# One GpSimd instruction for each token's second scatter factor

## The chip, the cores and the metric

The kernel runs on one core of a Trainium2 chip. The metric is the device time of one execution in microseconds (us). A core has five engines that run side by side, each through its own list of instructions in a fixed order: TensorE (PE, with its weight loads as PEld), VectorE (DVE), ScalarE (ACT), GpSimd (POOL) and SyncE (SP). SP, ACT and POOL also issue DMA transfers, and such an issue has its place in the engine's list.

## The reference, cut to what matters

The program is one decoder layer on 1,024 tokens of 1,024 features. A first half (projections, gating, a state space model, an output projection) ends in a residual `x`. The second half retrieves experts. Each token has 8 heads. For each head the token is scored against two lists of 128 keys, the best 16 of both lists give 16 experts out of 128 x 128, and a softmax gives their gates:

```
top_s, top_i = lax.top_k(s, PEER_TOPK)
cand_i = top_i[:, :, 0, :, None] * PEER_NKEYS + top_i[:, :, 1, None, :]
best_s, pos = lax.top_k(cand_s, PEER_TOPK)
idx = jnp.take_along_axis(cand_i, pos, axis=-1)
g = jax.nn.softmax(best_s, axis=-1)
act = jax.nn.gelu(jnp.einsum('thkd,td->thk', u_tab[idx], t))
return jnp.einsum('thk,thkd->td', g * act, v_tab[idx])
```

So each token has 128 slots (8 heads x 16), each with a row index i, a column index j (expert 128*i + j) and a gate g.

## The kernel before, in words

The tokens form eight blocks of 128. Blocks 5 to 7 take the sparse way: their experts' rows are gathered from memory by POOL's indirect DMAs (L871, L882), which run all through the last part of the program. Blocks 0 to 4 take the dense way: all 16,384 experts are computed for them by matmuls (`stage1`, tiles `pa`, and `stage2`, tiles `res` and `pd`), and each token's gates must first stand in a dense table `G_d` of 128 x 128 numbers for each token.

That table is made by `scatter`, the function that the change touches. For each token two factors are built, with the token's 128 slots on the partitions. `a1` has a one at column i of each slot (L679, one DVE instruction for four tokens). `b1` has the gate g at column j of each slot. One matmul of the two (L689, tile `pgs`, one for each token, two records in the trace) sums over the slots and gives the token's 128 x 128 table. ACT copies eight tokens' tables from PSUM to `GS` (L692), and SP writes `GS` to `G_d`. In 640 tokens (five blocks) this makes 160 `a1`, 640 `pgs` matmuls and 160 copies.

Before the change `b1` takes two steps. For eight tokens DVE makes a one-hot `hot` in 16-bit floats (L674). Then, for most pairs of tokens, ACT multiplies the one-hot by the gate, one instruction for each token (L687); for every 6th, 9th or 2nd pair, as the list `dv` in `CFG` says for the block, DVE does it for the pair (L683). There are six `b1` tiles of two tokens each, and two `a1` tiles of four.

Around the scatter runs `route`, DVE's search for the best keys of one block (`topk`: MAX8, FIND_INDEX8 and MATCH_REPLACE8 on tiles `m`, `ixs`, `scr`, `bs`, `po`, `ca`, then lookups on `mk`). Blocks 0 to 4 need their route before their scatter, blocks 5 to 7 need it for their gathers. When the last `GS` lies in `G_d`, the tables `Gt` are loaded, `weigh` multiplies them into the activations `w`, and `stage2` begins.

The order on each engine comes in two steps. The list `plan` in `CFG` gives each part of the work (r5 for route of block 5, s3 for scatter of block 3) a start and a length, which set the order in which the parts are written. Then a scheduler of the framework, which reckons with its own durations of the instructions, may move instructions within each engine's list. On the chip each engine keeps its list.

Of the kernel before, what the change touches and what calls it, by code (L numbers as in the profile page):

```python
# [15 lines left out]
AF = mybir.ActivationFunctionType  # L16
ALU = mybir.AluOpType
# [4 lines left out]
P = 128  # L22
# [15 lines left out]
NE = 128  # L38
QG = 4
FMAX = 3.0e38  # L40
CFG = dict(xo=[2, 3, 4, 0, 1], gt=3, ss=7, hs=2, b1=6, nw=11, raw=1, ngb=3, rows=6, lead=5, per=6, dv=[6, 9, 9, 2, 99], early=2,
           hp=600, eo=(2, 4), em={2: 'pppxx', 4: 'Xpp'}, seg=4, plan=dict(
    op0=(-238.2, 44.5), sb0=(-21, 248.8), m5=(-490.1, 3.4), r0=(234.1, 82.1), op1=(132.1, 27.3), op2=(292.7, 7.7),
    sb1=(310, 10.8), op3=(364.9, 36.8), r1=(301.9, 79), s0=(261.5, 137.5), sb2=(303.2, 61.7), zv=(372.6, 16.7),
# [3 lines left out]
    gt=(858.2, 122), rel=(739, 334), s4=(981.8, 131.5), r5=(916.4, 58.6), r6=(989.9, 124.6), ld=(776, 675.7),  # L48
# [47 lines left out]
@with_exitstack  # L96
def tile_hybrid_layer(ctx: ExitStack, tc: tile.TileContext, a, out, cfg=CFG):
    nc = tc.nc
    V, A, G, T = nc.vector, nc.scalar, nc.gpsimd, nc.tensor
# [70 lines left out]
    def slotS(shape, name, dt=F32):  # L170
        return sS.tile(shape, dt, tag="k8", name=name)
# [36 lines left out]
    early = {}  # L208
# [341 lines left out]
    ss = []  # L550
# [93 lines left out]
        bc2 = sm.tile([P, D], F32, tag="x", name="bc2", bufs=3)  # L644
        nc.scalar.dma_start(gt2_d, row_bcast(bc2, mod[5], "gt2"))

    gx = kp = sC = tk = iot = iot8 = None

    def slotC(shape, name, dt=F32):
        return sC.tile(shape, dt, tag="k8", name=name)  # L650

    def mid():
        nonlocal gx, kp, sC, tk, iot, iot8
        sB.release()
        gx = ctx.enter_context(tc.tile_pool(name="gx", bufs=1, side="left"))
        kp = tc.alloc_tile_pool(name="tk", bufs=1, side="left")
        sC = tc.alloc_tile_pool(name="sC", bufs=4, side="right")
        tk = topk_consts(tc, kp)
        iot = kp.tile([P, P], F32, name="iot")
        G.iota(iot, pattern=[[1, P]], base=0, channel_multiplier=0, allow_small_or_imprecise_dtypes=True)  # L660
        iot8 = kp.tile([P, P, 8], F16, name="iot8")
        G.iota(iot8, pattern=[[1, P], [0, 8]], base=0, channel_multiplier=0, allow_small_or_imprecise_dtypes=True)
        yield

    tops = {}

    def scatter(b, I32t, J16, gT):
        t0 = b * P
        for q in range(4):
            GS = [slotS([P, NE // 2, 32], f"GS{b}_{q}_{i}") for i in range(2)]  # L670
            for t8 in range(4):
                s1 = q * 32 + t8 * 8
                hot = kp.tile([P, P, 8], F16, tag="hs", name=f"hot{b}_{s1}", bufs=cfg["hs"])
                V.tensor_tensor(hot, iot8, bcast(J16[:, s1:s1 + 8], 1, P), op=ALU.is_equal)  # L674
                pg = bankB(f"pgs{b}_{s1}")
                for o in range(8):
                    if o % 4 == 0:
                        a1 = kp.tile([P, 4, P], F32, tag="a1", name=f"a1_{b}_{s1 + o}", bufs=2)
                        V.tensor_tensor(a1, bcast(iot, 1, 4), bcast(I32t[:, s1 + o:s1 + o + 4], 2, P), op=ALU.is_equal)  # L679
                    if o % 2 == 0:  # L680
                        b1 = kp.tile([P, 2, P], F32, tag="b1", name=f"b1_{b}_{s1 + o}", bufs=cfg["b1"])
                        if (s1 + o) // 2 % cfg["dv"][b] == 0:
                            V.tensor_tensor(b1, hot[:, :, o:o + 2].rearrange("p j t -> p t j"),  # L683
                                            bcast(gT[:, s1 + o:s1 + o + 2], 2, P), op=ALU.mult)
                        else:
                            for n in range(2):
                                A.activation(b1[:, n], hot[:, :, o + n], AF.Copy,  # L687
                                             scale=gT[:, s1 + o + n:s1 + o + n + 1])
                    T.matmul(pg[:, o // 4, (o % 4) * P:(o % 4 + 1) * P], b1[:, o % 2], a1[:, o % 4], start=True, stop=True)  # L689
                pgv = pg.rearrange("p a (t i) -> p i (a t)", t=4)  # L690
                for i in range(2):
# [58 lines left out]
    def route(b):  # L750
        if b < NDB:
            sc = scs.pop(b)
            get = lambda h: sc[:, h]
        else:
            part = {}

            def get(h):
                if h % 2 == 0:
                    part[0] = kp.tile([P, 2, 2, P], F32, tag="hs", name=f"scr{b}_{h}", bufs=cfg["hs"])
                    nc.sync.dma_start(part[0], sc_d[b - NDB, :, h:h + 2])  # L760
                return part[0][:, h % 2]

        i32, j16, g = yield from topk(tc, kp, tk, get, b)
        if b >= NDB:
            gi = gx.tile([P, NS], F32, name=f"gw{b}")
            ix = gx.tile([P, NS], I32, name=f"ix{b}")
            V.tensor_copy(gi, g)
            fi = kp.tile([P, NS], F32, tag="fi", name=f"fi{b}")
            V.scalar_tensor_tensor(fi, i32, 128.0, j16, op0=ALU.mult, op1=ALU.add)
            V.tensor_copy(ix, fi)  # L770
            tops[b] = ix, gi
        else:
            ij = kp.tile([P, 2, NS], F32, tag="ij", name=f"ij{b}")
# [262 lines left out]
    def prep_steps(n):  # L1036
# [17 lines left out]
        gt=(gt2_row, 1, "m5"), rel=(release, NDB, "gt op7 sb7"), ld=(lambda: lead(0, L), 2 * L, "rel"))  # L1054
# [13 lines left out]
    while left:  # L1068
# [3 lines left out]
        _, n, need = items[item]  # L1072
# [383 lines left out]
```

## Time and profile before

| what | value |
|---|---|
| median of 3 runs | 2688.28 us (2676.6 to 2693.47) |
| profiled execution, first to last instruction (span) | 2681.3 us |
| profiled execution's own time beside the span | none is given; the median run is 7.0 us above the span |
| PE busy | 2549.5 us, 95% |
| DVE busy | 2302.3 us, 86% |
| ACT busy | 903.2 us, 34% |
| POOL busy | 1038.4 us, 39% |

The busy shares are means over very different stretches. The scatter runs from 357 us (first `hot`) to 857.7 us (last copy to `GS`); after it comes the long loop over the experts, up to the end. POOL does nothing at all between 340 and 860 us, and its busy time is almost all in the loop's gathers. "Releaser" in a row is what ended an engine's idle time.

### The profile page before, as it was taken

What the parts mean: (1) busy time and instruction counts of PE and PEld (TensorE: products, weight loads), DVE (VectorE), ACT (ScalarE), POOL (GpSimd) and SP (SyncE); (2) the same over time, 40 slices, a digit from 0 to 9 for tenths busy, and PEclk for the clock granted to TensorE, in tenths of its full rate; (3) what the DMA queues carried; (4) which work ended last, traced back from release to release, by engine and by line L of the source; (5) the groups of instructions that cost most, each with busy time, mean ns of one, the idle gap of its engine ahead of it and who ended that gap; (6) DMA issues with size and microseconds to landing.
All of it is one profiled execution on the core that took longest, in us unless ns stands there. A gap on an engine that the chain in (4) does not pass through costs nothing.

```text
span 2681.3 us, 39165 instructions
## 1 busy us (share of the span) xinstructions
PE 2549.5 (95%) x14119; PEld 2171.5 (81%) x14119; DVE 2302.3 (86%) x5013; ACT 903.2 (34%) x1612; POOL 1038.4 (39%) x842
## 2 busy tenths in 40 slices
PE   6999999999878999999999999999999999999995
PEld 2557676588667898999889999888998899998894
DVE  7984699869899888888898988789897889888998
ACT  2311246578877422222222222222222222222222
POOL 0001000000000255566665665556565456555662
PEclk9996999999997999999999999999999999999998
DMA  9646232342545699999999999989999899998995
GB/s 351 114 151 181 101 134 103 111 157 111 200 139 198 236 348 316 324 330 330 330 359 342 344 332 324 331 312 345 335 341 333 301 330 368 336 332 305 353 322 201
DMA packets 298115, 724.76 MB, mean 270 GB/s; under 512 B 42384, under 2 KB 133008, under 8 KB 292384
## 3 DMA queue, kind: packets, MB, share of 16 engines
q0 software_dynamic: 112832, 411.09, 41.9%
q1 hardware_dynamic: 88800, 254.48, 26.6%
q10 hardware_dynamic: 96288, 56.69, 7.5%
q8 instruction: 111, 1.82, 0.3%
q14 instruction: 84, 0.69, 0.1%
HBM read 658.60 MB, written 62.39 MB: 269 GB/s over the span
## 4 chain that ended last, share of the span: by engine, by line
PE 24%; issue 23%; DVE 21%; POOL 15%; DMA 10%; ACT 5%; POOLq 0%; ACTq 0%; DVEq 0%
POOL rv L882 12%; PE pa L927 6%; DVE jk L874 4%; DMA Gt<-G_d 4%; PE pd L973 4%; POOL ru L871 3%; ACT b L687 3%; PE res L964 3%; PE pq L724 2%; PE po L626 2%; PE pgs L689 2%; DMA ru<-in_peer_u_dram,ix 1%; ACT GS L692 1%; PE pzs L360 1%; DMA vr<-in_peer_v_dram 1%
## 5 line engine op out<-in xcount | busy, mean ns | idle before, releaser
L927 PE MATMUL pa<-Th,u 128*128 128x320 f32 x4096 | 912.4, 310 | 8.7 <-DVE acc L981 5.3
L871 POOL DMA_INDIRECT ru<-in_peer_u_dram,ix x384 | 503.2, 1310 | 1016.4 <-issue 702.0
L927 PEld LDWEIGHTS pa<-Th,u 128*128 128x128 f32 x4096 | 688.3, 188 | 13.5 <-issue 3.3
L882 POOL DMA_INDIRECT rv<-in_peer_v_dram,ix x384 | 515.0, 1341 | 341.7 <-DVE gacc L887 271.1
L927 PE MATMUL pa<-Tl,u 128*128 128x320 f32 x2048 | 634.3, 310 | 0.0
L973 PE MATMUL pd<-v,wh 128*128 128x512 f32 x1536 | 482.4, 392 | 17.0 <-ACT v L913 6.9
L887 DVE SCALAR_TENSOR_TENSOR gacc<-rv,act,gacc 128x1024 f32<-128x1024 f32 x381 | 487.7, 1280 | 8.0 <-DMA rv<-in_peer_v_dram,ix 5.1
L874 DVE CUSTOM_DVE_ANT_0 jk<-ru,hn 128x1024 bf16<-128x1024 f32 x384 | 468.0, 1219 | 14.0 <-DMA ru<-in_peer_u_dram,ix 10.8
L927 PEld LDWEIGHTS pa<-Tl,u 128*128 128x128 f32 x2048 | 385.8, 188 | 1.2
L973 PEld LDWEIGHTS pd<-v,wh 128*128 128x128 f32 x1536 | 288.3, 189 | 81.8 <-ACT v L913 10.7
L964 PE MATMUL res<-v,wh 128*128 128x512 f32 x1024 | 319.4, 390 | 0.8 <-ACT wh L949 0.8
L973 PE MATMUL pd<-v,wl 128*128 128x512 f32 x768 | 299.9, 391 | 0.2 <-DVE wl L950 0.2
L946 DVE TENSOR_TENSOR w<-w,Gt 128x320 f32<-128x320 f32 x256 | 123.6, 483 | 184.7 <-DMA Gt<-G_d 181.4
L905 ACT CAST u<-ur 128x1024 fp32r<-128x1024 f32 x128 | 134.4, 1050 | 429.2 <-PE pd L973 231.1
L949 ACT CAST wh<-w 128x640 fp32r<-128x640 f32 x128 | 93.1, 728 | 492.7 <-DVE w L946 492.4
L687 ACT ACTIVATE b<-hot,gT 128x128 f32<-128x128 f16 x520 | 233.0, 536 | 59.5 <-PE pgs L689 40.2
L689 PE MATMUL pgs<-a,b 128*128 128x128 f32 x1280 | 191.0, 302 | 43.3 <-DVE a L679 21.0
L689 PEld LDWEIGHTS pgs<-a,b 128*128 128x128 f32 x1280 | 172.5, 210 | 65.2 <-ACT b L687 32.7
L964 PEld LDWEIGHTS res<-v,wh 128*128 128x128 f32 x1024 | 192.1, 188 | 40.7 <-ACT wh L949 1.2
L929 ACT ACTIVATE w<-pa 128x320 f32<-128x320 f32 x256 | 109.5, 434 | 281.5 <-PE pa L927 228.3
L964 PE MATMUL res<-v,wl 128*128 128x512 f32 x512 | 199.2, 390 | 1.4 <-DVE wl L950 1.4
L973 PEld LDWEIGHTS pd<-v,wl 128*128 128x128 f32 x768 | 144.8, 188 | 31.0 <-DVE wl L950 0.6
(348 smaller groups left out, 2994.5 us busy)
## 6 DMA issues: line engine op xcount, KB each, us to landing
vr<-in_peer_v_dram SPq DMA_DIRECT2D x128, 512.0 KB, 7.1
ur<-in_peer_ut_dram SPq DMA_DIRECT2D x128, 512.0 KB, 7.1
G_d<-GS SPq DMA_DIRECT2D x40, 1024.0 KB, 5.9
Gt<-G_d ACTq DMA_DIRECT2D x64, 640.0 KB, 16.4
wada<-in_w_ada_dram SPq DMA_DIRECT2D x17, 1024.0 KB, 13.3
wo<-in_w_out_dram SPq DMA_DIRECT2D x8, 1024.0 KB, 4.9
ru<-in_peer_u_dram,ix POOLq DMA_INDIRECT x384, 7.2
rv<-in_peer_v_dram,ix POOLq DMA_INDIRECT x384, 7.3
```

The costliest lines, as they stand in the source:

```text
L687: A.activation(b1[:, n], hot[:, :, o + n], AF.Copy, scale=gT[:, s1 + o + n:s1 + o + n + 1])
L689: T.matmul(pg[:, o // 4, (o % 4) * P:(o % 4 + 1) * P], b1[:, o % 2], a1[:, o % 4], start=True, stop=True)
L871: G.indirect_dma_start(out=row, out_offset=None, in_=a["peer_u"], in_offset=bass.IndirectOffsetOnAxis(ap=ix[:, s:s + 1], axis=0))
L874: V.tensor_tensor_reduce(out=junk, in0=row, in1=hn, scale=1.0, scalar=0.0, op0=ALU.mult, op1=ALU.add, accum_out=act[:, s:s + 1])
L882: G.indirect_dma_start(out=row, out_offset=None, in_=a["peer_v"], in_offset=bass.IndirectOffsetOnAxis(ap=ix[:, s:s + 1], axis=0))
L887: V.scalar_tensor_tensor(ac, row, act[:, s:s + 1], ac, op0=ALU.mult, op1=ALU.add)
L905: A.copy(u[:, 0], ur)
L927: T.matmul(pa[:, :NN], l[:, k, :], r[:, k, ns], start=(k == 0 and m == 0), stop=(k == KD - 1 and m == 2))
L929: A.activation(w[:, ns], pa[:, :NN], AF.Gelu_apprx_tanh)
L946: V.tensor_mul(w3, w3, Gt[i // QG][n][:, :, q * 32:(q + 1) * 32])
L964: T.matmul(res[tb][:, n, :], l[:, ts], r[:, n * 512:(n + 1) * 512], start=(g == 0 and q == 0 and m == 0), stop=(g == NGR - 1 and q == QG - ...
L973: T.matmul(po, l[:, ts], r[:, n * 512:(n + 1) * 512], start=(q == 0 and m == 0), stop=(q == QG - 1 and m == 2))
```

## The change

`hot` and its 16-bit iota go away, with the list `dv`. The column indices `Jt` are kept as 32-bit floats. `b1` is made by POOL, one instruction for each token: it compares the row 0..127 with the slot's index j and multiplies the result by the slot's gate, both of which are operands with one value for each partition.

```
-CFG = dict(..., rows=6, lead=5, per=6, dv=[6, 9, 9, 2, 99], early=2,
+CFG = dict(..., rows=6, lead=5, per=6, early=2,
...
-        iot8 = kp.tile([P, P, 8], F16, name="iot8")
-        G.iota(iot8, pattern=[[1, P], [0, 8]], base=0, channel_multiplier=0, ...)
...
-                hot = kp.tile([P, P, 8], F16, tag="hs", name=f"hot{b}_{s1}", bufs=cfg["hs"])
-                V.tensor_tensor(hot, iot8, bcast(J16[:, s1:s1 + 8], 1, P), op=ALU.is_equal)
                 pg = bankB(f"pgs{b}_{s1}")
                 for o in range(8):
...
                     if o % 2 == 0:
                         b1 = kp.tile([P, 2, P], F32, tag="b1", name=f"b1_{b}_{s1 + o}", bufs=cfg["b1"])
-                        if (s1 + o) // 2 % cfg["dv"][b] == 0:
-                            V.tensor_tensor(b1, hot[:, :, o:o + 2].rearrange("p j t -> p t j"),
-                                            bcast(gT[:, s1 + o:s1 + o + 2], 2, P), op=ALU.mult)
-                        else:
-                            for n in range(2):
-                                A.activation(b1[:, n], hot[:, :, o + n], AF.Copy,
-                                             scale=gT[:, s1 + o + n:s1 + o + n + 1])
+                        for n in range(2):
+                            c = s1 + o + n
+                            G.tensor_scalar(b1[:, n], iot, Jt[:, c:c + 1], gT[:, c:c + 1],
+                                            op0=ALU.is_equal, op1=ALU.mult)
                     T.matmul(pg[:, o // 4, (o % 4) * P:(o % 4 + 1) * P], b1[:, o % 2], a1[:, o % 4], ...)
...
-            Jt = kp.tile([P, P], F16, tag="Jt", name=f"Jt{b}", bufs=2)
+            Jt = kp.tile([P, P], F32, tag="Jt", name=f"Jt{b}", bufs=2)
```

The scheduler also moves instructions that the diff does not name. In the rows that follow, the first number in a name is the block (`a1_3_48` is block 3, tokens 48 to 51; `pgs4` is block 4; `mk6` belongs to route 6; `pa0` to expert group 0), the number at the end is only a count, and the two operands after the arrow are the inputs. Lines behind the scatter are 8 lower in the changed file.

DVE, where blocks 1 and 3 are scattered in turns. Before:

```order
L679 TENSOR_TENSOR a1_3_36_5395<-iot_1808,It3_4012 128x512
L674 TENSOR_TENSOR hot1_64_5439<-iot8_1810,Jt1_3132 128x1024
L683 TENSOR_TENSOR b1_3_44_5424<-hot3_40_5408,gT3_4014 128x256
L679 TENSOR_TENSOR a1_3_40_5411<-iot_1808,It3_4012 128x512
L679 TENSOR_TENSOR a1_3_44_5422<-iot_1808,It3_4012 128x512
L674 TENSOR_TENSOR hot3_48_5468<-iot8_1810,Jt3_4013 128x1024
L679 TENSOR_TENSOR a1_1_64_5442<-iot_1808,It1_3131 128x512
L683 TENSOR_TENSOR b1_3_48_5473<-hot3_48_5468,gT3_4014 128x256
L679 TENSOR_TENSOR a1_1_68_5454<-iot_1808,It1_3131 128x512
```

And in the changed kernel:

```order
L675 TENSOR_TENSOR a1_3_36_5335<-iot_1808,It3_3985 128x512
L1386 TENSOR_TENSOR mk6_6794<-mk6_6794 128x512
L759 COPY gw6_6897<-g6_6781 128x128
L1386 TENSOR_TENSOR mk6_6794<-mk6_6794 128x256
L1387 TENSOR_TENSOR ci6_6795<-mk6_6794 128x128
L1392 TENSOR_SCALAR i326_6856<-ci6_6795 128x128
L1393 TENSOR_SCALAR ci6_6795<-ci6_6795 128x128
L1395 TENSOR_TENSOR bp6_6859<-po6_6655,ci6_6795 128x128
L1378 TENSOR_TENSOR mk6_6794<-bp6_6859,tk_sx_1758 128x2048
L675 TENSOR_TENSOR a1_3_40_5350<-iot_1808,It3_3985 128x512
L1381 TENSOR_TENSOR mk6_6794<-mk6_6794,dd6_6791 128x2048
L1386 TENSOR_TENSOR mk6_6794<-mk6_6794 128x1024
```

Routes 5 and 6 now stand between these `a1`, almost whole between the 72nd and the 93rd `a1` of 160; before, both stood behind the 93rd. Right after the last rows of route 6 the changed list goes on with thirty `a1` in a row.

POOL, from the constants on. Before:

```order
L1328 MEMSET tk_sx_1758 128x128
L1329 MEMSET tk_sv_1759 128x1
L660 IOTA iot_1808 128x128
L662 IOTA iot8_1810 128x1024
L871 DMA ru0_0_7705<-in_peer_u_dram,ix5_6197 128x1024
```

And in the changed kernel, where 640 instructions (320 rows like these) stand ahead of the first gather `ru0_0`:

```order
L660 IOTA iot_1808 128x128
L680 TENSOR_SCALAR b1_0_0_2416<-iot_1808,Jt0_2339,gT0_2340 128x128 x2
L680 TENSOR_SCALAR b1_0_2_2421<-iot_1808,Jt0_2339,gT0_2340 128x128 x2
L680 TENSOR_SCALAR b1_0_4_2428<-iot_1808,Jt0_2339,gT0_2340 128x128 x2
L680 TENSOR_SCALAR b1_0_6_2433<-iot_1808,Jt0_2339,gT0_2340 128x128 x2
```

PE, at the last tokens of block 4. Before:

```order
L927 MATMUL pa1_0_7085<-Th_6646,u1_7081 128x320 x2
L927 MATMUL pa1_0_7085<-Tl_6647,u1_7081 128x320
L689 MATMUL pgs4_120_6965<-a1_4_124_6978,b1_4_124_6980 128x128 x2
L689 MATMUL pgs4_120_6965<-a1_4_124_6978,b1_4_126_6985 128x128 x2
L927 MATMUL pa1_0_7085<-Th_6646,u1_7081 128x320 x2
```

And in the changed kernel:

```order
L919 MATMUL pa2_0_7041<-Th_6560,u2_7037 128x320
L919 MATMUL pa2_0_7041<-Tl_6561,u2_7037 128x320
L681 MATMUL pgs4_120_6863<-a1_4_124_6876,b1_4_126_6883 128x128
L919 MATMUL pa2_0_7041<-Th_6560,u2_7037 128x320 x2
L919 MATMUL pa2_0_7041<-Tl_6561,u2_7037 128x320
L919 MATMUL pa2_0_7041<-Th_6560,u2_7037 128x320 x2
L681 MATMUL pgs4_120_6863<-a1_4_124_6876,b1_4_126_6883 128x128
```

The last 31 `pgs` now stand one at a time between `pa` matmuls, and 103 `pa` matmuls stand ahead of the last `pgs`; before there were 65.

## Rows read from the trace of the kernel before

**Rows 1.** The page's own line of busy time by engine.

```profile
PE 2549.5 (95%) x14119; PEld 2171.5 (81%) x14119; DVE 2302.3 (86%) x5013; ACT 903.2 (34%) x1612; POOL 1038.4 (39%) x842
```

**Rows 2.** Busy time by stretch: start and end, length, each engine's busy us, clock, DMA.

```profile
340.00:640.00 300.00, 292.18 (x1763) 220.19 (x1762) 266.18 (x1164) 192.36 (x422) 0.00 (x0) 0.99 0.34 124
640.00:680.00 40.00, 34.90 (x256) 32.04 (x254) 35.64 (x67) 35.65 (x81) 0.00 (x0) 0.91 0.39 159
680.00:860.00 180.00, 139.86 (x863) 120.64 (x863) 165.53 (x646) 146.92 (x325) 0.00 (x0) 0.88 0.45 165
...
1500.00:2000.00 500.00, 496.75 (x2786) 452.20 (x2786) 434.45 (x583) 121.11 (x175) 295.43 (x225) 1.00 0.93 332
```

**Rows 3.** The same by stretch for DVE's instructions on tile a1 alone.

```profile
340.00:640.00 300.00, 47.40 (x70) 0.99 0.34 124
640.00:680.00 40.00, 15.61 (x23) 0.91 0.39 159
680.00:860.00 180.00, 45.47 (x67) 0.88 0.45 165
```

**Rows 4.** The same for tile pgs: PE, PEld and ACT.

```profile
340.00:640.00 300.00, 74.79 (x560) 70.19 (x560) 37.32 (x70) 0.99 0.34 124
680.00:860.00 180.00, 90.16 (x545) 79.04 (x544) 37.92 (x71) 0.88 0.45 165
...
800.00:860.00 60.00, 33.28 (x160) 29.57 (x160) 11.68 (x22) 0.72 0.52 181
```

**Rows 5.** The scatter's instructions by line: busy us, mean ns, idle before.

```profile
L687 ACT ACTIVATE b<-hot,gT 128x128 f32<-128x128 f16 x520 | 233.0, 536 | 59.5 <-PE pgs L689 40.2
L674 DVE TENSOR_TENSOR hot<-iot,Jt 128x1024 f16<-128x1024 f16 x80 | 54.6, 684 | 11.4 <-ACT b L687 11.4
L683 DVE TENSOR_TENSOR b<-hot,gT 128x256 f32<-128x256 f16 x60 | 36.1, 607 | 3.4 <-PE pgs L689 3.0
```

**Rows 6.** Waits from 340 to 860 us: us in total, times, longest.

```profile
PEld pgs L689 <- ACT b L687: 32.7, 29, 2.7
...
PE pgs L689 <- DVE a L679: 21.0, 23, 2.4
```

**Rows 7.** DVE's lines from 680 to 860 us: a1, hot, b1, and one of route's.

```profile
L679 DVE TENSOR_TENSOR a<-iot,It 128x512 f32<-128x512 f32 x67 | 45.5, 682 | 1.6 <-PE pgs L689 1.5
L674 DVE TENSOR_TENSOR hot<-iot,Jt 128x1024 f16<-128x1024 f16 x32 | 21.9, 684 | 4.0 <-ACT b L687 4.0
L683 DVE TENSOR_TENSOR b<-hot,gT 128x256 f32<-128x256 f16 x25 | 14.8, 606 | 0.2
L1342 DVE FIND_INDEX8 ixs<-m,scr 128x8 uint16<-128x128 f32 x40 | 10.8, 285 | 0.0
L825 DVE TENSOR_TENSOR Tl<-t,Th 128x1024 fp32r<-128x1024 f32 x5 | 6.0, 1214 | 0.0
L906 DVE TENSOR_TENSOR u<-ur,u 128x1024 fp32r<-128x1024 f32 x3 | 3.6, 1214 | 0.2 <-ACT u L905 0.2
```

**Rows 8.** POOL's lines that come nearest to the new instruction.

```profile
L871 POOL DMA_INDIRECT ru<-in_peer_u_dram,ix x384 | 503.2, 1310 | 1016.4 <-issue 702.0 <-DVE act L874 277.3 <-DVE wl L950 16.1
L1327 POOL MEMSET tk_st<- 128x128 int16 x16 | 3.2, 202 | 43.0 <-DMA ys_d<-Yg 43.0
L516 POOL TENSOR_SCALAR_AFFINE_SELECT cst<-cst 128x128 f32<-128x128 f32 x4 | 1.2, 336 | 34.1 <-DMA cst<-in_w_s_dram 34.1
```

**Rows 9.** The chain of waits at the scatter's end and in the loop: start, us, what.

```profile
856.69 0.96 ACT GS L692 x2
...
858.03 5.35 DMA G_d<-GS
...
863.45 8.52 DMA Gt<-G_d
...
916.48 28.16 PE pa L927 x192
```

More of the change, by code (lines that the diff above doesn't have):

```diff
@@ L40 @@
 FMAX = 3.0e38
-CFG = dict(xo=[2, 3, 4, 0, 1], gt=3, ss=7, hs=2, b1=6, nw=11, raw=1, ngb=3, rows=6, lead=5, per=6, dv=[6, 9, 9, 2, 99], early=2,
+CFG = dict(xo=[2, 3, 4, 0, 1], gt=3, ss=7, hs=2, b1=6, nw=11, raw=1, ngb=3, rows=6, lead=5, per=6, early=2,
            hp=600, eo=(2, 4), em={2: 'pppxx', 4: 'Xpp'}, seg=4, plan=dict(
@@ L645, in late_gt2 @@
         nc.scalar.dma_start(gt2_d, row_bcast(bc2, mod[5], "gt2"))
-    gx = kp = sC = tk = iot = iot8 = None
+    gx = kp = sC = tk = iot = None
     def slotC(shape, name, dt=F32):
@@ L652, in mid @@
     def mid():
-        nonlocal gx, kp, sC, tk, iot, iot8
+        nonlocal gx, kp, sC, tk, iot
         sB.release()
@@ L660, in mid, with scatter @@
         G.iota(iot, pattern=[[1, P]], base=0, channel_multiplier=0, allow_small_or_imprecise_dtypes=True)
-        iot8 = kp.tile([P, P, 8], F16, name="iot8")
-        G.iota(iot8, pattern=[[1, P], [0, 8]], base=0, channel_multiplier=0, allow_small_or_imprecise_dtypes=True)
         yield
     tops = {}
-    def scatter(b, I32t, J16, gT):
+    def scatter(b, I32t, Jt, gT):
         t0 = b * P
@@ L681, in scatter @@
                         b1 = kp.tile([P, 2, P], F32, tag="b1", name=f"b1_{b}_{s1 + o}", bufs=cfg["b1"])
-                        if (s1 + o) // 2 % cfg["dv"][b] == 0:
-                            V.tensor_tensor(b1, hot[:, :, o:o + 2].rearrange("p j t -> p t j"),
-                                            bcast(gT[:, s1 + o:s1 + o + 2], 2, P), op=ALU.mult)
-                        else:
-                            for n in range(2):
-                                A.activation(b1[:, n], hot[:, :, o + n], AF.Copy,
-                                             scale=gT[:, s1 + o + n:s1 + o + n + 1])
+                        for n in range(2):
+                            c = s1 + o + n
+                            G.tensor_scalar(b1[:, n], iot, Jt[:, c:c + 1], gT[:, c:c + 1], op0=ALU.is_equal, op1=ALU.mult)
                     T.matmul(pg[:, o // 4, (o % 4) * P:(o % 4 + 1) * P], b1[:, o % 2], a1[:, o % 4], start=True, stop=True)
```

## The prediction

> **What bounds the kernel now.** I read the page's busy line first, then busy time by stretch, because the busy line averages over stages that have different limits: PE shows 95% there, DVE 86%, ACT 34%, POOL 39% [rows 1]. By stretch [rows 2], the loop over the experts (the row of 1500 to 2000 us stands for it) has PE busy 496.75 of 500 us. None of the edited instructions runs there, so the loop's length should stay, and the question is when it can begin. It begins when the last gate table has been copied, at about 857.7 us, and has gone to memory and back: the write takes 5.35 us and the load 8.52 us [rows 9].
>
> The scatter before it has three pieces. From 340 to 640 us PE is busy 292 of 300 us [rows 2]: PE sets the pace, and what I take from DVE or ACT buys little. 70 of the 160 `a1` are done there [rows 3]. From 640 to 680 us DVE and ACT are both busy 36 of 40 us, for 23 `a1`. From 680 to 860 us DVE is busy 165.5 of 180 us, ACT 146.9, PE only 139.9, for the other 67 `a1`, or 268 tokens. So in the last 220 us PE waits for factors. The waits agree: PE's weight loads waited 32.7 us for ACT's `b1` and PE waited 21.0 us for DVE's `a1` [rows 6].
>
> **What goes.** DVE loses 80 `hot` (54.6 us) and 60 `b1` (36.1 us), 90.7 us in all; ACT loses 520 `b1`, 233.0 us [rows 5]. Of DVE's 90.7 us, 21.9 + 14.8 = 36.7 us lie behind 680 us [rows 7]. Most of the rest lies under the PE bound, where I cost it at nothing: the cover is PE's 292 us, and PE's work does not change. The longer `Jt` is the same copy with wider output, and the dropped 16-bit iota ran long before anyone needed it: nothing for both.
>
> **What is added.** 640 POOL instructions on an engine that is busy 0.00 us in all three pieces [rows 2]. The trace has no such instruction, so I bound its price from POOL's own rows [rows 8]. Below: a MEMSET of the same width, 0.20 us, which reads nothing. Above: the gather, 1.31 us, a different thing altogether. Nearest: the affine select on 128x128 32-bit floats, 0.336 us, which reads one tile, compares and picks. The new one reads the same amount, does two operations and takes two operands by partition. I put it between one such select and two, 0.34 to 0.67 us, and take 0.50 us, an estimate. To that I add a share of `a1`: DVE spends 45.5 us on 67 of them, 0.17 us for each token, and I do not expect POOL to hand over tokens without ever losing some time to what runs beside it. With 0.15 us for that, the working price is **0.65 us a token**.
>
> The Trainium skill, page GPSIMD Engine Reference, section Performance versus the Vector engine, gives 769 ns for 512 elements in a tight loop; by that 128 elements would be about 0.2 us plus dispatch, which is an estimate, and the sum would be that of the first rival below. No row here shows a POOL compare of that kind; the select's 0.336 us is above it.
>
> **What is moved.** The changed DVE list has routes 5 and 6 in front of the 93rd `a1`, about 1.6 routes of them behind the 72nd. A route is 28 us of DVE: from 680 to 860 us DVE's 165.5 us less 45.5 (`a1`), 21.9 (`hot`), 14.8 (`b1`), 6.0 and 3.6 (the loop's first tiles) and some 5 us of other work leave 69 us, in which 40 of route's L1342 ran, at 16 a route 2.5 routes [rows 7]. So the second piece is now 23 `a1` (15.6 us, [rows 3]) and 1.6 routes (45 us): 61 us where 40 were taken. It begins at 640 us, since PE bounds what is ahead, and ends at 701 us. On SP the table writes keep their order, with the route's loads of blocks 5 and 6 ahead of the writes of blocks 1 and 3; these loads wait for nothing late. On POOL the first gather now stands behind all 640 instructions, but its indices and buffers come free only in the loop's first part, so no price.
>
> **The sum.** Behind 701 us the changed DVE list is `a1` after `a1`, 67 or 68 of them, so 272 tokens are left. Three engines could pace them. DVE has 45.5 us of `a1`, one route and about 15 us more, near 90 us. PE had 139.9 us of work in that piece before; at the 0.134 us of the first piece in place of 0.165 us for each `pgs` record [rows 4], 545 records would be 73 instead of 90 us, so PE needs 123 us. POOL needs 272 x 0.65 = 177 us. POOL decides, and six `b1` tiles let it run only 12 tokens ahead. The scatter then ends at 701 + 177 = 878 us, 20 us later than 857.7. Of this I take back 6 us: 103 in place of 65 `pa` matmuls are already done by then, at 28.16/192 = 0.147 us each [rows 9]. What is late next is the same write and load of the last table. Result: +14 us. The span goes from 2681.3 to about 2695 us. The page gives no time of its own for the profiled execution; the median of the runs shown, 2688.3, is 7.0 us above the span, so I predict **2702 us**, 0.5% more. Less than 1%, about 27 us, cannot be told from no change here.
>
> The formula for the rest is: change = 272 x price - 157 - 6, with a floor where PE paces (123 us in place of the product). Even lies at 0.60 us, one per cent faster at 0.50, one per cent slower at 0.70.
>
> **Rival 1, POOL is cheap: faster.** If the price is 0.34 to 0.45 us, PE paces the tail and the floor holds: 123 - 163 = -40 us, 2648 us. For it: the one select in the trace costs 0.336 us, and POOL has nothing else to do. Against it: two operations and two operands by partition. It needs a price under 0.50 us in practice.
>
> **Rival 2, POOL and DVE get in each other's way: slower.** The place is the tail, where every `a1` reads two tiles while POOL reads its own. If the two reads exclude each other and the instruction costs 0.67 us, a token costs 0.67 + 0.17 = 0.84 us: 228 - 163 = +65 us, 2753 us; at 1.0 us a token +109 us. It decides from 0.70 us on. For it: nearly everything DVE does here is two-tile work. Against it: POOL is idle in these pieces now, so no row shows such a loss. The Trainium skill has this rule on the page SBUF — State Buffer, section Who interferes with whom: a DVE instruction with two SBUF inputs and a GpSimd instruction that reads SBUF block each other for their whole length. No run here shows it yet.
>
> **Rival 3, nothing to see.** PE's busy time might hide that the last pieces are paced by something else, and the edit moves only idle time: 2688 us.
>
> **How the numbers follow.** I give my forecast (0.57 to 0.73 us a token, -8 to +36 us) 0.38, rival 1 0.28, rival 2 0.29, rival 3 0.05. The forecast's own range is 2680 to 2724. Rival 1 counts as faster by over 1% except for a twentieth part: 0.26. Rival 2 is slower: 0.29, and the forecast adds 0.07 at its upper end, 0.36. The same: 0.38. The range for 8 in 10 takes rival 1 to its floor and rival 2 to 1.0 us: 2646 to 2795 us.
>
> **What would show it.** In the profile of the changed kernel: the POOL rows of L680, with the spacing of two in a row (0.5 alone, 0.65 with all) and who waits for `b1`: in the tail PE should wait for POOL, and POOL hardly for PE. `a1` number 93 should start near 701 us, the last `GS` copy should be near 878 us, and from there to the first `pd` the time should be some 6 us less than before. DVE's `a1` should keep their 0.68 us; if they are longer, or POOL's spacing is wider where `a1` run, rival 2 is at work. If POOL waits for PE in the tail, rival 1. I am wrong altogether if the loop behind changes its length, or if the first piece, up to 640 us, gets longer or shorter by more than 10 us.

## The result: 4.8% slower, outside the range

The changed kernel takes 2822.23 us in the median of four runs (2806.05 to 2826.01), the kernel before 2682.44 us in the median of four (2668.51 to 2693.47). The ratio is 1.0479, 95% interval 1.0441 to 1.0516: slower, where I had forecast no change that can be told, and above the top of my range. The profiled executions have spans of 2823.4 and 2681.3 us, 142.1 us apart. All of what follows is about where these 142 us arise.

### The profile page after: what moved, and what is told of

Its sections match the earlier page's. It is cut to its first block, busy times and chain, and to the rows that moved or that the text cites. A ratio compares the mean times of both kernels' runs of the same rounds, so it can differ in the third digit from the quotient of the medians.

```text
span 2823.4 us, 39122 instructions
## 1 busy us (share of the span) xinstructions
PE 2654.5 (94%) x14119; PEld 2228.5 (79%) x14119; DVE 2245.1 (80%) x4873; ACT 688.8 (24%) x1090; POOL 1638.8 (58%) x1481
## 4 chain that ended last, share of the span: by engine, by line
POOL 25%; issue 21%; PE 20%; DVE 18%; DMA 12%; ACT 1%; ACTq 0%; POOLq 0%; DVEq 0%; SPq 0%
POOL b L680 12%; POOL rv L874 7%; POOL ru L863 5%; DMA Gt<-G_d 5%; DVE gacc L879 4%; PE pa L919 3%; DMA ru<-in_peer_u_dram,ix 3%; PE po L626 3%; PE pd L965 3%; DVE jk L866 2%; DMA rv<-in_peer_v_dram,ix 2%; PE res L956 2%; PE pzs L360 2%; PE pq L716 1%; PE pgs L681 1%
## 5 line engine op out<-in xcount | busy, mean ns | idle before, releaser
L863 POOL DMA_INDIRECT ru<-in_peer_u_dram,ix x384 | 513.5, 1337 | 367.7 <-DVE act L866 283.7
L874 POOL DMA_INDIRECT rv<-in_peer_v_dram,ix x384 | 508.7, 1325 | 363.7 <-DVE gacc L879 294.2
L680 POOL TENSOR_SCALAR b<-iot,Jt,gT 128x128 f32<-128x128 f32 x640 | 598.3, 951 | 137.4 <-ACT gT L777 99.1
L965 PE MATMUL pd<-v,wh 128*128 128x512 f32 x1536 | 483.5, 393 | 35.7 <-ACT wh L941 18.8
L866 DVE CUSTOM_DVE_ANT_0 jk<-ru,hn 128x1024 bf16<-128x1024 f32 x384 | 468.2, 1219 | 18.0 <-DMA ru<-in_peer_u_dram,ix 14.5
L681 PE MATMUL pgs<-a,b 128*128 128x128 f32 x1280 | 303.1, 367 | 71.4 <-DVE a L675 37.4
L681 PEld LDWEIGHTS pgs<-a,b 128*128 128x128 f32 x1280 | 232.1, 247 | 140.9 <-POOL b L680 123.3
L675 DVE TENSOR_TENSOR a<-iot,It 128x512 f32<-128x512 f32 x160 | 115.1, 721 | 167.5 <-PE pgs L681 167.5
```

Source lines behind the costliest of these rows:

```text
L680: G.tensor_scalar(b1[:, n], iot, Jt[:, c:c + 1], gT[:, c:c + 1], op0=ALU.is_equal, op1=ALU.mult)
L863: G.indirect_dma_start(out=row, out_offset=None, in_=a["peer_u"], in_offset=bass.IndirectOffsetOnAxis(ap=ix[:, s:s + 1], axis=0))
L866: V.tensor_tensor_reduce(out=junk, in0=row, in1=hn, scale=1.0, scalar=0.0, op0=ALU.mult, op1=ALU.add, accum_out=act[:, s:s + 1])
L874: G.indirect_dma_start(out=row, out_offset=None, in_=a["peer_v"], in_offset=bass.IndirectOffsetOnAxis(ap=ix[:, s:s + 1], axis=0))
L965: T.matmul(po, l[:, ts], r[:, n * 512:(n + 1) * 512], start=(q == 0 and m == 0), stop=(q == QG - 1 and m == 2))
```

## The profile after

The page's busy line, to set against [rows 1]: POOL has 600 us more, DVE and ACT have less, PE has 105 us more with the same number of instructions.

```profile
PE 2654.5 (94%) x14119; PEld 2228.5 (79%) x14119; DVE 2245.1 (80%) x4873; ACT 688.8 (24%) x1090; POOL 1638.8 (58%) x1481
```

Busy time by stretch, columns as in [rows 2] (start and end, length, PE, PEld, DVE, ACT, POOL, clock, DMA):

```profile
340.00:640.00 300.00, 292.01 (x1748) 217.09 (x1747) 228.39 (x1064) 86.13 (x165) 250.90 (x263) 0.99 0.32 116
640.00:680.00 40.00, 20.92 (x94) 18.24 (x91) 38.73 (x195) 8.57 (x19) 40.00 (x42) 0.56 0.31 109
680.00:860.00 180.00, 146.51 (x499) 104.50 (x499) 100.15 (x392) 32.16 (x61) 176.42 (x200) 0.59 0.24 97
860.00:1000.00 140.00, 118.39 (x600) 96.71 (x599) 74.56 (x274) 40.83 (x69) 135.98 (x142) 0.71 0.41 141
1500.00:2000.00 500.00, 497.97 (x2800) 453.90 (x2800) 435.55 (x597) 126.44 (x183) 296.66 (x223) 1.00 0.94 335
```

The scatter, which had ended at 857.7 us, now lasts until 996 us. From 640 us on POOL is busy nearly without a gap, DVE six tenths of the time, ACT under a quarter. PE's busy time is misleading here: the granted clock is 0.56 to 0.71, and at 0.59, near the lower of its two levels (1.2 and 2.4 GHz), 499 instructions fill 146 us where 863 filled 140 us before. The loop behind (last row) looks as it did.

PE alone, where the clock fell (start and end, length, busy us and count, clock, DMA):

```profile
630.00:640.00 10.00, 10.00 (x90) 1.00 0.10 39
640.00:645.00 5.00, 2.13 (x18) 0.95 0.33 133
645.00:650.00 5.00, 3.53 (x14) 0.50 0.67 181
```

PE first ran out of work (2.13 of 5 us, waiting for POOL's and DVE's factors), and then stood at the lower level. So here the low clock came after the waiting. That it does not set the pace POOL shows: from 640 us to the end of the scatter it was idle for PE only three times, 3.6 us together.

POOL's new instruction by line: busy us, mean ns, idle before it and what ended that. PE's matmuls and weight loads and DVE's `a1` stand below it.

```profile
L680 POOL TENSOR_SCALAR b<-iot,Jt,gT 128x128 f32<-128x128 f32 x640 | 598.3, 951 | 137.4 <-ACT gT L777 99.1 <-PE pgs L681 38.4
L681 PE MATMUL pgs<-a,b 128*128 128x128 f32 x1280 | 303.1, 367 | 71.4 <-DVE a L675 37.4 <-POOL b L680 24.6 <-DVE bs L1336 3.0
L681 PEld LDWEIGHTS pgs<-a,b 128*128 128x128 f32 x1280 | 232.1, 247 | 140.9 <-POOL b L680 123.3 <-issue 15.9
L675 DVE TENSOR_TENSOR a<-iot,It 128x512 f32<-128x512 f32 x160 | 115.1, 721 | 167.5 <-PE pgs L681 167.5
```

POOL waited 38.4 us for PE over the whole scatter (the 99.1 us lie ahead of its start but for half a microsecond); PE's two queues (matmuls and weight loads) waited 148 us for POOL. Before, they waited 44 us for ACT's factors, 32.7 on the weight loads [rows 6] and 11.4 on the matmuls, whose row before is:

```profile
L689 PE MATMUL pgs<-a,b 128*128 128x128 f32 x1280 | 191.0, 302 | 43.3 <-DVE a L679 21.0 <-ACT b L687 11.4 <-ACT GS L692 4.3
```

POOL's mean of 951 ns hides two populations. The same line, its shortest, median and longest instruction in ns, and its first and last start:

```profile
L680 POOL TENSOR_SCALAR b<-iot,Jt,gT x640: 782/793/3439, 353.8 to 990.2; 128x128 f32<-128x128 f32 x160
```

More than half take about 0.79 us; 137 take over 1 us, the longest 3.44 us. Two pieces of POOL's timeline show which (start, us, what):

```profile
741.93 6.77 POOL L680 TENSOR_SCALAR b<-iot,Jt,gT 128x128 f32<-128x128 f32 x5
...
794.78 5.52 POOL L680 TENSOR_SCALAR b<-iot,Jt,gT 128x128 f32<-128x128 f32 x7
```

And DVE in the first of these two pieces, with one of its `a1` of the second at the end:

```profile
742.04 1.41 DVE L1378 TENSOR_TENSOR mk<-bp,tk_sx 128x2048 int16<-128x2048 int16 x1
743.37 0.68 DVE L675 TENSOR_TENSOR a<-iot,It 128x512 f32<-128x512 f32 x1
743.98 1.21 DVE L1381 TENSOR_TENSOR mk<-mk,dd 128x2048 int16<-128x2048 int16 x1
745.22 1.28 DVE L1386 TENSOR_TENSOR mk<-mk 128x1024 int16<-128x1024 int16 x2
746.43 0.68 DVE L675 TENSOR_TENSOR a<-iot,It 128x512 f32<-128x512 f32 x1
...
796.45 0.85 DVE L675 TENSOR_TENSOR a<-iot,It 128x512 f32<-128x512 f32 x1 [2.33 <-PE pgs L681]
```

Beside work of this kind, which reads two tiles, POOL made 5 factors in 6.77 us, 1.35 us each. At 795 us, where DVE did two `a1` in 5 us, it made 7 in 5.52 us, 0.79 each; there it was the `a1` that took longer, 0.85 us in place of 0.68. Over all 640, sorted by what DVE did meanwhile: 157 ran beside an idle DVE, mean 0.791 us, longest 0.805; 119 beside DVE instructions with one tile alone (nearly all of them the searches of `topk`), mean 0.797; 364 beside at least one that reads two tiles, mean 1.071.

Where the time went, piece by piece. POOL's `b1` and DVE's `a1` up to the starts of `a1` 71 and 94, and to the scatter's end (length, busy us and count, clock, DMA); first POOL, then DVE's `a1`, then all engines in the second piece (columns as in [rows 2]):

```profile
353.70:663.60 309.90, 274.50 (x286) 0.96 0.34 123
663.60:749.30 85.70, 85.31 (x86) 0.52 0.27 105
749.30:996.20 246.90, 238.51 (x270) 0.67 0.31 112
```

```profile
353.70:663.60 309.90, 48.28 (x70) 0.96 0.34 123
663.60:749.30 85.70, 15.91 (x23) 0.52 0.27 105
749.30:996.20 246.90, 50.90 (x67) 0.67 0.31 112
```

```profile
663.60:749.30 85.70, 49.74 (x211) 44.35 (x212) 83.08 (x427) 14.63 (x29) 85.31 (x86) 0.52 0.27 105
```

In the second piece DVE is as full as POOL: 83.1 of 85.7 us, of which `a1` takes 15.9 and mostly the routes that moved forward take the rest.

Behind the scatter: the first gather, the last copies to `GS` and the table load in the changed kernel (start, us, what), then the first and last start of `pd`, before and after:

```profile
993.96 2.11 POOL ru L863
...
995.04 1.06 ACT L684 COPY GS<-pgs 128x512 f32<-128x512 f32 x2
...
1007.47 12.62 ACTq L930 DMA_DIRECT2D Gt<-G_d  x3
```

```profile
L973 PE MATMUL pd<-v,wh x1536: 387/389/793, 887.3 to 2660.9; 128*128 128x512 f32 x192
...
L965 PE MATMUL pd<-v,wh x1536: 387/389/793, 1028.4 to 2810.7; 128*128 128x512 f32 x192
```

## The experiments

The theory after this reading: GpSimd's 640 instructions set the pace of the whole scatter, by a lone price (the time of one when nothing blocks it) of about 0.77 us, longer than I allowed for, and by stalls while VectorE reads two tiles. The rivals: the routes that moved forward on VectorE did it; or any busy VectorE lengthens GpSimd's work; or it is the mix of engines and not the price. Ratios are against the kernel before in runs on the same chip. The scheduler orders each version anew, so the order on DVE and PE differs from version to version as well; only the control and the test of the second try below have the same order.

**The price by itself, and what blocks what.** A kernel of stages, each of 24 GpSimd instructions alone or beside another engine's:

```
stage("both", p_both(P), None)              # compare and multiply, alone
stage("one", p_one, None)                   # compare only
stage("wide", p_both(512), None)            # 512 columns
stage("dboth", None, d_both)                # the same on VectorE
stage("bwtwo", p_both(P), d_two)            # beside a1
stage("bwpsum", p_both(P), d_psum)          # beside a1 with its iota in PSUM
stage("bwcol", p_both(P), d_col, nd=64)     # beside compares with a column
...
```

> Nothing of the layer is computed: stages of 24 instructions, each begun when the one before has ended, for prices and for what blocks what. Theory (GpSimd and a VectorE instruction with two tiles in SBUF exclude each other): compare-and-multiply of 128 columns alone 0.774 us from start to start, 0.58 with one operation; beside back-to-back a1 of two tiles GpSimd's takes 1.2 us or more; beside the same a1 with one of its tiles in PSUM, beside VectorE's compare with a column, and beside ScalarE's copies it keeps 0.774; a GpSimd memset beside a1 keeps its lone time. Rival (any busy VectorE lengthens it): longer beside the PSUM form and the column form as well. The first kernel with a1 by column leaves open what the column form does: 313 instructions beside it and other one-tile work took 0.845 us on average.

POOL by line (busy us, mean ns):

```profile
L99 POOL TENSOR_SCALAR po_wide<-src_wide,Jc_wide 128x512 f32<-128x512 f32 x24 | 49.3, 2071 | 2.7 <-ACT Jc_wide L75 2.7
L99 POOL TENSOR_SCALAR po_bwint<-src_bwint,Jc_bwint 128x128 f32<-128x128 f32 x24 | 38.0, 1597 | 3.1 <-ACT Jc_bwint L75 3.1
L99 POOL TENSOR_SCALAR po_bwtwo<-src_bwtwo,Jc_bwtwo 128x128 f32<-128x128 f32 x24 | 27.9, 1176 | 36.1 <-ACT Jc_bwtwo L75 36.1
L99 POOL TENSOR_SCALAR po_bwcopy<-src_bwcopy,Jc_bwcopy 128x128 f32<-128x128 f32 x24 | 23.6, 995 | 3.1 <-ACT Jc_bwcopy L75 3.1
L99 POOL TENSOR_SCALAR po_bwcol<-src_bwcol,Jc_bwcol 128x128 f32<-128x128 f32 x24 | 20.7, 876 | 3.1 <-ACT Jc_bwcol L75 3.1
L99 POOL TENSOR_SCALAR po_both<-src_both,Jc_both 128x128 f32<-128x128 f32 x24 | 18.6, 791 | 3.3 <-ACT Jc_both L75 3.3
L99 POOL TENSOR_SCALAR po_bwpsum<-src_bwpsum,Jc_bwpsum 128x128 f32<-128x128 f32 x24 | 18.6, 791 | 3.1 <-ACT Jc_bwpsum L75 3.1
L99 POOL TENSOR_SCALAR po_bwact<-src_bwact,Jc_bwact 128x128 f32<-128x128 f32 x24 | 18.6, 791 | 3.1 <-ACT Jc_bwact L75 3.1
L103 POOL TENSOR_SCALAR po_one<-src_one,Jc_one 128x128 f32<-128x128 f32 x24 | 13.9, 600 | 2.7 <-ACT Jc_one L75 2.7
```

And DVE in three of the stages: `a1` beside POOL, `a1` alone, and the compare-and-multiply on DVE.

```profile
L109 DVE TENSOR_TENSOR do_bwtwo<-src_bwtwo,Jc_bwtwo 128x512 f32<-128x512 f32 x24 | 15.2, 707 | 2.6 <-ACT Jc_bwtwo L75 2.6
L109 DVE TENSOR_TENSOR do_dtwo<-src_dtwo,Jc_dtwo 128x512 f32<-128x512 f32 x24 | 14.5, 685 | 93.2 <-ACT Jc_dtwo L75 93.2
...
L118 DVE TENSOR_SCALAR do_dboth<-src_dboth,Jc_dboth 128x128 f32<-128x128 f32 x24 | 6.2, 341 | 2.6 <-ACT Jc_dboth L75 2.6
```

Alone, 24 take 18.6 us, 0.774 each. With the compare only they take 13.9 us, 0.58 each, and with 512 columns 49.3 us, 2.05 each. A second operation thus costs 0.19 us, and 384 more columns cost 1.28 us: 0.0033 us a column and 0.35 us that do not depend on the width. DVE does 24 compare-and-multiplies of 128 columns in 6.2 us, 0.26 each.

Beside `a1` POOL's 24 took 27.9 us, DVE's 15.2 instead of 14.5. POOL's mean of 1176 ns mixes two stretches again, because DVE's 24 were done after 15 us. POOL's share of both (length, busy us and count, clock, DMA):

```profile
131.46:146.50 15.04, 15.04 (x8) 1.00 0.00 0
146.50:159.40 12.90, 12.88 (x17) 1.00 0.00 0
```

While `a1` followed `a1`, POOL finished 8 instructions, 1.90 us from start to start, about three `a1`; after that it needed 0.774 again. So beside back-to-back `a1` its price is not half as much again but two and a half times the lone one. POOL lost 9.3 us in all and DVE 0.7, so in this stage it is nearly always POOL that waits. With one of `a1`'s tiles in PSUM (the second on-chip memory; the other tiles lie in SBUF) POOL lost nothing, and beside ACT nothing. So a busy DVE is not enough. But the theory in its narrow form missed: DVE's compare with a column and its copy, one tile each, lengthened POOL's instruction too. Their means of 876 and 995 ns are diluted in the same way: while DVE ran, it was mostly 0.91 us beside the compare and 1.53 us beside the copy. The memsets of POOL ran ahead of the `a1` meant to stand beside them, so that stage tells nothing.

Two pages of the Trainium skill bear on this. SBUF — State Buffer, section Who interferes with whom, has GpSimd and VectorE share one pair of ports as an exclusive lock, taken by VectorE instructions with two inputs in SBUF, and by copies and tensor-scalar instructions such as the compare with a column where these run in a two-port mode; the rows agree on which instructions block, with 1.91 us beside `a1`, 1.53 and 0.91 beside these, 0.79 where an input was in PSUM. That each side blocks the other for its whole length, as the prediction quoted the rule, they do not show: VectorE lost 0.7 us to the eight GpSimd instructions beside it, under 0.1 us each. GPSIMD Engine Reference, section Performance versus the Vector engine, which the prediction quoted for 769 ns at 512 elements in a tight loop, does not give this instruction's time: 2.05 us measured.

**The order of the routes.** The kernel before, one-hot and planner as they were, with every multiply on GpSimd:

```
+ for n in range(2):
+     c = s1 + o + n
+     G.tensor_scalar(b1[:, n], hot[:, :, o + n], gT[:, c:c + 1], None, op0=ALU.mult)
```

> The kernel before with its one-hot on VectorE and its order of routes (5 and 6 behind the 119th a1), but every multiply on GpSimd, one instruction a token. Theory (GpSimd's price sets the pace, and the order that moved is no cause): the scatter ends as late as in the changed kernel or later, since VectorE reads two tiles for the one-hot too: 2810 to 2860 us. Rival (the routes that moved forward made the loss): near the kernel before, 2680 to 2720 us. If a multiply alone is cheaper than compare and multiply, this lies between.

2851.82 us, 1.0571 (1.0496 to 1.0645). The routes stand where they stood before, and it is slower than the change. So a loss of this size needs no moved routes. What their move costs inside the changed kernel, where they fill DVE in the second piece, no run isolates. Its rows:

```profile
L684 POOL TENSOR_SCALAR b<-hot,gT 128x128 f32<-128x128 f16 x640 | 563.0, 900 | 193.3 <-DVE hot L674 135.0 <-PE pgs L685 53.4 <-DVE sm L1366 3.6
...
L674 DVE TENSOR_TENSOR hot<-iot,Jt 128x1024 f16<-128x1024 f16 x80 | 65.2, 816 | 46.9 <-POOL b L684 46.7
```

POOL waits for DVE's one-hot and DVE's one-hot for POOL (`hot` has two buffers), and `hot` itself takes 816 instead of 684 ns [rows 5]: here DVE loses too.

**Compare without multiply.** The changed kernel, `op1` and the gate left out, so the tables hold ones for gates:

```
- G.tensor_scalar(b1[:, n], iot, Jt[:, c:c + 1], gT[:, c:c + 1], op0=ALU.is_equal, op1=ALU.mult)
+ G.tensor_scalar(b1[:, n], iot, Jt[:, c:c + 1], None, op0=ALU.is_equal)
```

> The changed kernel with the compare alone on GpSimd; the multiply by the gate is left out, so the table holds ones for gates. Tells what the 0.774 us from start to start are made of. Theory A (each of the two operations has its pass over 128 elements): a lone instruction falls to about 0.4 us, GpSimd no longer sets the pace, and the time falls to 2650 to 2700 us. Theory B (the time goes by instruction and elements, whatever is done with them): still 0.77 us, 2810 to 2830 us.

2749.64 us, 1.0207 (1.0137 to 1.0277): between the two theories.

```profile
L680 POOL TENSOR_SCALAR b<-iot,Jt 128x128 f32<-128x128 f32 x640 | 476.0, 762 | 191.0 <-ACT gT L777 98.3 <-PE pgs L681 74.6 <-ACT Jt L776 18.1
```

The lone price falls by 0.19 us, 640 of them by 124 us; POOL's busy time falls by 122 and the median by 73 us against the change. The rest went into waits: POOL now idles 74.6 us for PE in place of 38.4, and 18 us for `Jt`. So a lower price on POOL shortens the program, and some six tenths of it are paid back; the order of the routes moved here as well.

**Less blocking, first try.** `a1` as four compares with a column:

```
- V.tensor_tensor(a1, bcast(iot, 1, 4), bcast(I32t[:, s1 + o:s1 + o + 4], 2, P), op=ALU.is_equal)
+ for n in range(4):
+     V.tensor_scalar(a1[:, n], iot, I32t[:, s1 + o + n:s1 + o + n + 1], None, op0=ALU.is_equal)
```

> The changed kernel with a1 made of four VectorE instructions that read one tile and a column, in place of one that reads two tiles. Theory (GpSimd waits while VectorE reads two tiles): of the 102 us by which the changed kernel's POOL instructions are longer than their lone 0.791 us, the 49 us that fall beside a1 go; the mean falls from 0.951 to about 0.87 us and the time from 2822 to about 2775 us, although VectorE spends about 60 us more on a1. Rival (POOL's long instructions have another cause, such as a busy VectorE of any kind, or PE's pace): mean stays at 0.95 or more, 2815 to 2840 us.

2817.82 us, 1.0444 (1.0364 to 1.0524), not told apart from the change. POOL's mean fell to 907 ns, where the theory had 0.87 us and the rival 0.95. The column form blocks as well, as the stages showed, and `a1` became longer: PE waited 53.5 us for it in place of 37.4. A test that did not take away what it meant to.

**Less blocking, second try.** Here `a1` reads its iota from PSUM. That needs a PSUM bank, so a control has three banks in the pool of four and nothing else:

```
+ iop = psI.tile([P, 512], F32, name="iop")
+ V.tensor_copy(iop[:, 0:P], iot)
- V.tensor_tensor(a1, bcast(iot, 1, 4), bcast(I32t[:, s1 + o:s1 + o + 4], 2, P), op=ALU.is_equal)
+ V.tensor_tensor(a1, bcast(iop[:, 0:P], 1, 4), bcast(I32t[:, s1 + o:s1 + o + 4], 2, P), op=ALU.is_equal)
```

> Control for the next run: the changed kernel with three PSUM banks in the pool of single banks in place of four, which makes room for a bank that holds the iota. No theory of GpSimd speaks of it; it may cost some per cent anywhere. POOL's instructions should keep their mean of about 0.95 us.

> The control with a1's iota in PSUM, so that a1 reads one tile in SBUF and one in PSUM; nothing else differs. Theory (GpSimd waits while VectorE reads two tiles in SBUF, and GpSimd sets the pace): the 49 us of blocking that fall beside a1 go, the mean of a POOL instruction falls from 0.95 to about 0.87 us, and since a1 keeps its 0.68 us the time falls by 30 to 49 us against the control. Rival (the blocked time would turn into waits elsewhere, as when a1 was made by column): within 10 us of the control.

The control took 2819.62 us (2816.99 to 2824.52), the test 2800.79 us (2800.37 to 2811.04): 18.8 us less, and no run of the one reaches into those of the other, though the ratios' intervals overlap (1.0472, 1.0435 to 1.0509, and 1.0418, 1.0379 to 1.0457). POOL's row of the control, and then POOL's and DVE's of the test:

```profile
L680 POOL TENSOR_SCALAR b<-iot,Jt,gT 128x128 f32<-128x128 f32 x640 | 592.5, 942 | 134.9 <-ACT gT L777 92.9 <-PE pgs L681 42.0
```

```profile
L683 POOL TENSOR_SCALAR b<-iot,Jt,gT 128x128 f32<-128x128 f32 x640 | 544.3, 864 | 156.5 <-ACT gT L780 93.2 <-PE pgs L684 63.2
...
L678 DVE TENSOR_TENSOR a<-iop,It 128x512 f32<-128x512 f32 x160 | 108.8, 681 | 152.5 <-PE pgs L684 152.3
```

POOL lost 48.2 us of busy time, the 49 expected, and `a1` went back from 722 to 681 ns. Every engine has the same order in both. So `a1` against POOL is a cause, shown in the kernel itself, of about 19 of the 142 us. The time fell by less than forecast because 21 of the 48 us came back as POOL's wait for PE.

**More look-ahead.** The changed kernel with `b1=9` in place of `b1=6`:

> The changed kernel with nine b1 tiles in place of six, 18 tokens of look-ahead. Theory: GpSimd idled 38 us for PE, all but 3 us of it before 640 us, and each idle stretch shrinks by up to 6 x 0.77 = 4.6 us: 10 idle stretches, 10 to 30 us less than 2822, so 2792 to 2815 us. Rival (PE's waits for GpSimd's single late tokens, not GpSimd's idle time, set the end): no change, 2815 to 2830 us.

2814.51 us, 1.0482 (1.0434 to 1.053) where the change had 1.0479: not told apart. POOL idled 28.5 us for PE in place of 38.4, so the idle time is a small part.

**A smaller share on GpSimd.** Half (of each eight tokens four on GpSimd, the one-hot four columns wide), a quarter, and only the pairs that VectorE had multiplied:

```
+ if o >= 4:                     # the quarter: o >= 6; the pairs: (s1 + o) // 2 % cfg["dv"][b] == 0
+     for n in range(2):
+         c = s1 + o + n
+         G.tensor_scalar(b1[:, n], iot, Jf[:, c:c + 1], gT[:, c:c + 1], op0=ALU.is_equal, op1=ALU.mult)
+ else:
      for n in range(2):
          A.activation(b1[:, n], hot[:, :, o + n], AF.Copy, scale=gT[:, s1 + o + n:s1 + o + n + 1])
```

> Of each eight tokens four by GpSimd as in the change, four by a one-hot of four columns on VectorE and ScalarE's multiply. Theory (it is the sum of GpSimd's prices that set the pace): 320 x 0.95 = 304 us of GpSimd fit into the 500 us of the scatter, VectorE is rid of its 36 us of b1 and about 20 us of one-hot: 2650 to 2685 us, at or under the kernel before. Rival (GpSimd at work costs VectorE or the order more than its own instructions take): 2710 us or more.

> As the half, but GpSimd has two tokens of each eight: 160 x about 1.0 = 160 us of GpSimd. Theory (in the half GpSimd's share of a tile of eight tokens, 4 x 1.04 us with stalls of up to 6 us, was what PE waited for): the loss shrinks; VectorE is rid of 36 us of b1 and about a quarter of the one-hot, so 2665 to 2700 us. Rival (every use of GpSimd beside two-tile work costs VectorE more than it saves): as late as the half, 2715 us or more.

> The kernel before, with its one-hot and ScalarE's 520 multiplies, but the 60 pairs that VectorE multiplied by GpSimd, one instruction a token: 120 x 1.0 = 120 us of GpSimd, 36 us less on VectorE of which 15 lie in its bound tail. Theory (a small share on GpSimd hides): 2670 to 2700 us, no loss. Rival (stalls of GpSimd behind two-tile work reach PE whatever the share): 2710 us or more.

2723.19, 2709.89 and 2713.0 us: 1.0108 (1.0076 to 1.014), 1.0109 (1.0066 to 1.0153) and 1.0105 (1.0059 to 1.0152). Four fifths of the loss are gone once POOL has spare time, but none of the three gains. My theory missed all three times: the half and the pairs lie in the rival's range, the quarter between both. POOL's row of the half:

```profile
L685 POOL TENSOR_SCALAR b<-iot,Jf,gT 128x128 f32<-128x128 f32 x320 | 330.3, 1044 | 292.3 <-PE pgs L690 156.9 <-ACT gT L788 97.5 <-PE pmx L533 19.2
```

POOL idles 157 us for PE, and PE's two queues waited 78 us for POOL all the same; the half's scatter ended at 883.4 us, 26 us later than before. My reading, argued and not tested: a factor that comes late by a stall (the longest took 6.2 us) holds up PE, and later idle time does not give that back. The quarter is another case. PE's two queues waited 4.5 us for POOL there, and the scatter ended at 856.9 us, no later than before. Of the 20.9 us by which its profiled execution is longer, 15.4 lie behind the first `pd`, in the loop that the edit does not touch (1809.3 us, before 1793.9). Why the loop is longer stays open.

**The same share on VectorE.** The quarter with `V.tensor_scalar` in place of `G.tensor_scalar`, and the change with it for all 640:

> The quarter again (two tokens of each eight by compare-and-multiply, the rest by a one-hot of six columns and ScalarE) with those two on VectorE, 0.257 us each from start to start in the stage by itself, in place of GpSimd. VectorE: 160 x 0.257 + 80 x 0.55 = 85 us where the kernel before has 90.7; ScalarE 480 multiplies where it has 520. Theory (what cost the quarter its 1.1% was GpSimd's late tokens): level with the kernel before or a little under, 2665 to 2690 us. Rival (the mix, or the order that the planner makes of it, cost it): 2705 us or more, as the quarter on GpSimd.

> The changed kernel with the same instruction on VectorE for every token. 640 x 0.257 = 164 us more on VectorE, which was busy 442 us between 340 and 1000 us of the changed kernel, and 74 us more than the kernel before has for the same factors; nothing blocks. Theory (price and blocking belong to GpSimd): VectorE paces the tail, between the two kernels, 2710 to 2770 us. Rival (one long instruction per token, on whatever engine, is what costs): 2800 us or more.

The quarter took 2706.14 us, 1.0055 (1.0029 to 1.0081), a little over the kernel before and not under it, at the edge of the rival's range. Its scatter too ended as early as before (857.1 us), and its loop too was longer (1809.5 us). So the quarter's loss in the loop does not need GpSimd; whether GpSimd adds to it stays open, since the two intervals overlap. All on VectorE took 2759.86 us, 1.0245 (1.0201 to 1.0288), about half the loss of the change.

```profile
L680 DVE TENSOR_SCALAR b<-iot,Jt,gT 128x128 f32<-128x128 f32 x640 | 186.7, 336 | 26.6 <-PE pgs L681 26.3
```

It adds 187 us to the engine that bounded the tail, 96 more than the 91 that went away, and still beats POOL's 598 us. No version here beats the kernel before.

## Why the prediction was wrong, step by step

The prediction had the right engine in the tail (POOL, not PE or DVE) and the wrong price, it let that price act on too few tokens, and it took the moved routes for shorter than they are.

- **The price, 0.50 us alone and 0.15 us of interference: failed, and it is the main step.** Alone it is 0.774 us, above both ends that I set (0.34 and 0.67) and above the 0.70 us from which I had called it slower. The stalls add 103 us in all (POOL's busy time 598.3 us less 640 x 0.774 = 495.4), 0.16 us a token, which is the size of my second term. I chose the affine select [rows 8] as the nearest row, and its 0.336 us was no guide, nor was the gather's 1.31 us. The price alone does not explain the miss: with the tail's measured 0.91 us my formula gives 272 x 0.91 - 163 = +85 us, 2773 us, still inside my range.
- **The tail: 272 tokens took 246.9 us, 0.91 us each, not 177 us.** 70 us of the miss.
- **The second piece: failed.** I reckoned it by DVE's list, 61 us. It took 85.7 us, and both lists were full: POOL was busy for 85.3 of them (92 tokens at 0.93) and DVE for 83.1. DVE's other work is 67 us there, where I had 45 for 1.6 routes at 28 us each. That price was too low, in part because the stretch that I took it from held the first search of 2.5 routes (the 40 L1342 on `ixs`), but of the later search on `po` only 16, at 8 a route two routes' worth. By this count most of these 25 us would have come with a cheap POOL too.
- **The first piece, costed at nothing under PE's 292 us: failed.** PE is as busy as before, but the 71st `a1` starts at 663.6 in place of 640.4 us. POOL needed 310 us for 280 tokens: 217 at the lone price, the rest stalls and its waits for PE. 23 us, more than the 10 us that I had named as the point from which I would be wrong.
- **The 6 us taken back: failed, small.** From the last table copy to the first `pd` it is 32.3 us (996.1 to 1028.4), before 29.7 (857.7 to 887.3): 3 us more, where I had 6 less. PE had run out of `pa` matmuls at about 1013 us and stood idle for 15.2 us until the first `wh` for `pd` was there. ACT was held for 12.6 us by issuing three loads of the tables. POOL's first gather, which I had put into the loop's first part at no price, started at 994.0 us, 34 us ahead of the first `pd`; before, it started 26 us behind it. Whether the early gathers delayed the table loads, no run tests.
- **The loop keeps its length: right.** From the first `pd` to the end 1795.0 us, before 1793.9.

Together 70 + 25 + 23 are the 118 us by which the scatter ended later than my 878 us; with 14 forecast, 9 for the 6 us not taken back, and 1 of the loop they make the 142 us.

Seen the other way, the scatter took 637 us on POOL: 495 at the lone price, 103 of stalls, 38 of idling for PE. The old scatter took 501 us in all. The lone price alone would have filled it, so even without a single stall there was next to nothing to win.

**The rivals.** Rival 2 is nearest to what happened: a price above 0.67 us, `a1` is longer (721 ns), POOL's spacing widens beside it. At its 1.0 us a token it gave +109 us; it fell short because it, too, charged the tail's 272 tokens alone and not all 640. Rival 1 (cheap) is refuted by the lone 0.774 us. Rival 3 is refuted by PE's waits for POOL.

## What to carry to other kernels

Before moving a per-item step to an engine, multiply its price by all items and hold the product against the whole stage: 640 x 0.774 us was already the old stage's length, and a bound for the last piece alone misses that. An engine that shows no busy time is cheap only per instruction that it is quick at: GpSimd's compare-and-multiply took three times VectorE's. And where VectorE works on two tiles beside it, charge GpSimd's stalls as well; moving one operand to PSUM takes that part away. Before trusting a mean, ask whether what ran beside it lasted as long: the 1176 ns beside `a1` were 1.91 us and then 0.79.

## What the runs showed of the hardware that was not expected

- GpSimd's price goes by operation and by column: 0.58 us with one operation and 0.77 with two at 128 columns, 2.05 us at 512.
- Beside back-to-back `a1` the loss is one-sided: GpSimd lost 9.3 us and VectorE 0.7, and GpSimd's instruction took 1.90 us from start to start in place of 0.774. Where single `a1` came, in the tail of the change, VectorE lost as well (0.85 in place of 0.68 us), and so did its one-hot (816 in place of 684 ns). In single cases GpSimd's instruction took 3.4 us in the change and 6.2 in the half.
- With one operand of `a1` in PSUM the block is gone entirely: 791 ns for every GpSimd instruction of that stage.
- With PE waiting, its granted clock fell to 0.59 from 680 to 860 us (0.88 before), and its busy share was 81% (146.51 of 180 us), higher than the 78% before, with 499 instructions in place of 863.
